# First MLP of a streaming encoder: eight instead of ten hidden pairs done plainly on the first token half, their order, and the places of the operand sums' steps

## The chip, the cores and the metric

One core of a Trainium2 chip. The metric is device time in microseconds of one execution. The kernel before took 2438.1 us, the median of 3 runs (2436.41 to 2440.5).

## The reference

Two trunk layers over 1056 tokens (1024 of a prompt, 32 of a sample), width 1024. Each layer is a mixer (layer 0 an mLSTM, layer 1 chunk-band attention), a residual LayerNorm, an MLP and a residual LayerNorm, with shift, scale and gate from a conditioning vector. The change touches the MLP of layer 0:

```python
x = layer_norm(ALPHA * x + (1 + g1) * y, p['ln_g'][l, 0], p['ln_b'][l, 0])
u = x * (1 + sc2) + sh2
f = jnp.square(jax.nn.relu(u @ p['w_up'][l])) @ p['w_down'][l]
x = layer_norm(ALPHA * x + (1 + g2) * f, p['ln_g'][l, 1], p['ln_b'][l, 1])
```

w_up is 1024 x 4096, w_down 4096 x 1024. All is in 32 bits: every operand is split into a high and a low part, and a product is three matmuls (high-high, high-low, low-high).

## The kernel before

Tokens lie along the free axis, features on the partitions. The 1056 tokens of the MLP are two halves of 528 (`tp` 0 and 1), each two quarters of 264 (QN). The 4096 hidden features are 16 pairs of 256 (`pb`), a pair being two blocks of 128. The upward product is done in two ways (function `mlp7`, lines 1103 to 1533).

*Plain.* For a pair on one half, four tiles (`up_tile`, L1159: block f, quarter q) of 8 k-steps with three matmuls each (`proj`, L118 to L120), 24 matmuls of 128 x 264 columns a tile, 96 a pair. The weights of a pair are two blocks of 512 x 256 (`up_weights`, `wblock`): loaded (L96) into a raw tile, cast to the high part on ScalarE (L89), the low part subtracted on VectorE (L90). ScalarE applies Relu to each tile (L1166), then squares the four (L1141), casts them into HL (L89), VectorE subtracts the low part (L90), and SyncE stores HL to DRAM (`hpl`, L1147).

*In seven products.* A unit (class `Seven`) treats a pair on one half as a 2 x 2 block product with seven multiplications instead of eight: 7 products of 12 matmuls (L1280), 84 a unit. PRODS says what each product multiplies and which of three PSUM tiles of the unit it adds into: the products 0, 2, 4 and 6 add into tile 0, product 1 into tile 1, products 3 and 5 into tile 2. After products 0, 2 and 3 ScalarE copies the PSUM tile to H (L1283), after 1, 4 and 5 VectorE adds it to H (L1286), after 6 ScalarE takes Relu (L1290). The weight forms of a pair (`forms`, four sums L1244 to L1247 of two raw tiles and seven splits, L89 and L90) serve both halves. The operands need sums of quarters of u (`tforms`, L1180): for each half, T3 into `ext` or `exu`, T1 and T2 into TF, and a last difference written in place into U, every step three or two subtractions on VectorE (L1190, L1191, L1195) and a split. It is a generator of six steps; a line in `mlp7` says after which plain tiles a step is taken.

*The order.* Pairs in FIRST (6 to 15) are plain on the first half, which is ready first; the first three of them fill the time in which the second half's LayerNorm ends, the other seven (`rest`) that of the operand sums: a table keyed by `at` (the plain tile pair, counted so that 13 is the last) says which generator moves: 0 or 1 the sums of the first or second half, 2 the weight forms of the first pair. Then come the units in the order of SEQ: a pair of FIRST has one unit (second half), the others two, 22 in all. Two neighbouring units are interleaved: product i of unit j stands at 7j + 2i. While the units run, 8 loads and VectorE work for the adaLN columns of the second layer are spread among them (`ada_some`, L1573, tiles `rada` and `aacc`). Last comes the downward product, in eight groups of two pairs (`dn_plain`), in the order `order_p`.

All raw tiles (weight blocks, `rdn` for the forms, the sums' `t`, `rada`) come from one ring of 3 (`raw_tile`). The weights as used come from a ring of 6 (`wc`), of which `exu` holds one. All DMAs named here are issued by SyncE in one queue. In the rows below a name ends in a buffer number; H_15_0 is pair 15 on half 0, t_0_1 the sum of layer 0, half 1, w_up_15_1 the second weight block of pair 15.

## Time and profile before

| | us |
|---|---|
| median of 3 runs | 2438.1 |
| the profiled execution | 2437.59 |
| its span, first to last instruction | 2435.8 |
| plain part of the first MLP (first matmul 514.0, last 631.4) | 117.5 |
| the 22 units (631.5 to 863.4) | 231.8 |
| TensorE busy | 2363.6 |
| VectorE busy | 1987.5 |
| ScalarE busy | 1178.8 |

The table by stage gives for each stretch the busy time of each engine and its instructions in brackets. The rows in order of time give the start, the duration, the engine, the line, the operation, what it writes and reads, the shape and the count; a bracket at the end is the idle time of the engine before it and what ended it. Matmuls overlap, so their cadence is read from starts. Times are counted from the span's start.

### The profile page before, as it was taken

To read this page: it belongs to the slowest core of one execution; us is meant where nothing else is said; L and a number is where in the kernel's file an instruction comes from. 1 tells how busy PE (TensorE), PEld (TensorE's weight loads), DVE (VectorE), ACT (ScalarE), POOL (GpSimd) and SP (SyncE) were. 2 spreads that over 40 slices of the span, in tenths; PEclk is the share of its full clock that TensorE was granted. 3 is DMA by queue.
4 is the path that set the end of the run, shared out by engine and by line. 5 is a ranking of instruction groups with operands and counts; after the bars stand their busy time and mean duration, and the time that the engine had idled before them with its cause. 6 is when DMAs were issued, how large, how long until landed. Compare 5 with 4: busy or idle time off the path is not lost.

```text
span 2435.8 us, 44452 instructions
## 1 busy us (share of the span) xinstructions
PE 2363.6 (97%) x17180; PEld 2265.8 (93%) x17180; DVE 1987.5 (82%) x4222; ACT 1178.8 (48%) x2394; POOL 166.6 (7%) x315
## 2 busy tenths in 40 slices
PE   7999999999999999999999999999999999899997
PEld 4999999999999999999989977889999999899997
DVE  4899898788788789999697666755998888887778
ACT  4644456278566620010157566763776777222212
POOL 0211100000000000000001134420000000000003
PEclk9999999999999999999999999999999999999999
DMA  8433223436556897656423220051486779966642
GB/s 297 128 103 98 82 86 102 158 113 215 182 186 194 296 343 266 234 203 232 143 64 97 74 64 1 11 133 36 162 279 233 252 255 341 367 242 232 229 151 72
DMA packets 292151, 423.61 MB, mean 174 GB/s; under 512 B 15576, under 2 KB 221804, under 8 KB 286820
## 3 DMA queue, kind: packets, MB, share of 16 engines
q1 hardware_dynamic: 287908, 390.50, 48.3%
q10 hardware_dynamic: 4032, 30.28, 3.1%
q8 instruction: 135, 2.21, 0.4%
q14 instruction: 76, 0.62, 0.1%
HBM read 304.91 MB, written 118.17 MB: 174 GB/s over the span
## 4 chain that ended last, share of the span: by engine, by line
PE 47%; DVE 12%; DMA 5%; ACT 4%; issue 2%; POOL 1%; SPq 0%; DVEq 0%; ACTq 0%; POOLq 0%
PE dn L1415 11%; PE up L1280 9%; PE dn L120 5%; PE dn L119 5%; PE dn L118 5%; PE pv L1853 3%; PE s L1796 2%; PE pt L1831 2%; DMA rdn_u<-in_w_up_dram 1%; DVE wf_u L90 1%; PE op_b L118 1%; PE op_b L119 1%; PE op_b L120 1%; DVE HL L90 1%; DMA radw<-in_w_ada_dram 1%
## 5 line engine op out<-in xcount | busy, mean ns | idle before, releaser
L1045 DVE SCALAR_TENSOR_TENSOR ACX<-dn,ada,ACX 128x264 f32<-128x264 f32 (+6 forms) x664 | 281.9, 448 | 86.4 <-PE dn L1415 41.4
L1415 PE MATMUL dn<-fx,wf_d 128*128 128x264 f32 x2016 | 254.0, 285 | 6.5 <-DVE ACX L1045 3.5
L1415 PEld LDWEIGHTS dn<-fx,wf_d 128*128 128x128 f32 x2016 | 248.7, 188 | 8.7 <-issue 2.5
L89 ACT CAST w_dn<-raw_dn 128x1024 fp32r<-128x1024 f32 x36 | 37.7, 1050 | 284.1 <-DVE aw L274 172.8
L118 PE MATMUL dn<-hs,w_dn 128*128 128x384 f32 (+2 forms) x512 | 161.3, 316 | 0.8 <-DVE ACX L1045 0.7
L119 PE MATMUL dn<-hs,w_dn 128*128 128x384 f32 (+2 forms) x512 | 160.9, 315 | 0.0
L120 PE MATMUL dn<-hs,w_dn 128*128 128x384 f32 (+2 forms) x512 | 155.9, 314 | 1.8 <-DVE w_dn L90 1.8
L1280 PE MATMUL up<-TF,wf_u 128*128 128x264 f32 x1056 | 143.6, 285 | 1.8 <-ACT H L1283 1.8
L1280 PE MATMUL up<-u,wf_u 128*128 128x264 f32 x1056 | 139.7, 285 | 1.7 <-DVE H L1286 0.8
L1280 PE MATMUL up<-U,wf_u 128*128 128x264 f32 x1056 | 139.6, 285 | 1.6 <-DVE H L1286 1.0
L274 DVE SCALAR_TENSOR_TENSOR aw<-radw,cs,aw 128x512 f32<-128x512 f32 x196 | 139.5, 745 | 0.0
L1280 PEld LDWEIGHTS up<-TF,wf_u 128*128 128x128 f32 x1056 | 134.3, 188 | 3.1 <-ACT H L1283 3.0
L1280 PEld LDWEIGHTS up<-U,wf_u 128*128 128x128 f32 x1056 | 133.1, 188 | 2.7 <-DVE H L1286 1.9
L1280 PEld LDWEIGHTS up<-u,wf_u 128*128 128x128 f32 x1056 | 132.6, 188 | 2.7 <-ACT wf_u L89 0.8
L119 PE MATMUL dn<-U,w_dn 128*128 128x384 f32 (+2 forms) x416 | 129.8, 313 | 0.0
L118 PE MATMUL dn<-U,w_dn 128*128 128x384 f32 (+2 forms) x416 | 129.3, 311 | 0.0
L120 PE MATMUL dn<-U,w_dn 128*128 128x384 f32 (+2 forms) x416 | 125.6, 312 | 0.9 <-DVE w_dn L90 0.9
L238 DVE SCALAR_TENSOR_TENSOR ada_room<-ada_room,cs 128x256 f32<-128x256 f32 x224 | 98.9, 476 | 4.2 <-DMA ada_room<-in_w_ada_dram 4.2
L120 PEld LDWEIGHTS dn<-hs,w_dn 128*128 128x128 f32 x512 | 95.8, 188 | 2.9 <-DVE w_dn L90 2.6
L118 PEld LDWEIGHTS dn<-hs,w_dn 128*128 128x128 f32 x512 | 96.4, 188 | 1.5 <-DVE ACX L1045 1.0
L119 PEld LDWEIGHTS dn<-hs,w_dn 128*128 128x128 f32 x512 | 96.5, 188 | 0.0
L1806 DVE CUSTOM_DVE_ANT_0 p<-s,bias 128x576 f32<-128x576 f32 (+9 forms) x132 | 79.1, 606 | 20.3 <-PE s L1796 13.4
(394 smaller groups left out, 7171.5 us busy)
## 6 DMA issues: line engine op xcount, KB each, us to landing
hpl<-HL SPq DMA_DIRECT2D x144, 264.0 KB
rdn_u<-in_w_up_dram SPq DMA_DIRECT2D x64, 512.0 KB
hd<-HL SPq DMA_DIRECT2D x28, 1056.0 KB
fx<-hd SPq DMA_DIRECT2D x50, 528.0 KB
radw<-in_w_ada_dram SPq DMA_DIRECT2D x24, 1024.0 KB
hd<-HM SPq DMA_DIRECT2D x28, 792.0 KB
raw_up<-in_w_up_dram SPq DMA_DIRECT2D x40, 512.0 KB
raw_dn<-in_w_down_dram SPq DMA_DIRECT2D x36, 512.0 KB
```

Source lines behind the costliest of these rows:

```text
L90: (eng or nc.vector).tensor_sub(dst_l, src, dst_h.bitcast(F32))
L118: nc.tensor.matmul(ps, wh, mov(0, k), start=(k == 0), stop=False)
L119: nc.tensor.matmul(ps, wh, mov(1, k), start=False, stop=False)
L120: nc.tensor.matmul(ps, wl, mov(0, k), start=False, stop=(k == nk - 1))
L238: nc.vector.scalar_tensor_tensor(acc[:, cnd], raw[:, k], sc, acc[:, cnd], op0=ALU.mult, op1=ALU.add)
L274: nc.vector.scalar_tensor_tensor(acc[cnd], raw[:, k], sc, acc[cnd], op0=ALU.mult, op1=ALU.add)
L1045: nc.vector.scalar_tensor_tensor(xs, ps[:, off + o:off + o + mm_], gate[:, fc, cnd:cnd + 1], xs, op0=ALU.mult, op1=ALU.add)
L1280: nc.tensor.matmul(p, self.ws[w][:, wl, k], moving(f, tp, xl, k), start=first and k + n_ == 0, stop=k == 3 and n_ == 2, skip_group_check=n ...
L1415: nc.tensor.matmul(p, ws[w][:, wl, k], t[:, s0, xl], start=first and k + n_ == 0, stop=k == kg - 1 and n_ == 2, skip_group_check=not first)
L1796: nc.tensor.matmul(s[:, b, :w], qst, kk[i][:, g, k0 + j0:k0 + j0 + w], start=(i == 0), stop=(i == 1))
L1806: nc.vector.tensor_tensor_reduce(out=z.rearrange("p (b w) -> p b w", b=np_), in0=s[:, :np_, :w], in1=bt.rearrange("p (b w) -> p b w", b=np ...
L1853: nc.tensor.matmul(pv[64 * e:64 * e + 64, :nq], V[:kp, vt0 + j, g * 64:(g + 1) * 64], pts[e][:kp, j, :nq], start=(j == 0), stop=(j == nt - 1))
```

## The change

```diff
@@ -1321,7 +1321,7 @@
-        order_p, blocks_p = (0, 3, 1, 4, 2, 5, 7, 6), [(q * QN, QN) for q in range(4)]
+        order_p, blocks_p = L.order, [(q * QN, QN) for q in range(4)]
@@ -1373,8 +1373,7 @@
                 at = 2 * j + f - 2 * len(rest) + 14
                 if at == 11:
                     prep(0)
-                for n in {2: (1,), 3: (1,), 4: (1,), 5: (1,), 6: (1,), 7: (1,), 8: (0,), 9: (0,), 11: (0, 2),
-                          12: (2,), 13: (2, 0)}.get(at, ()):
+                for n in L.at.get(at, ()):
                     if n < 2:
                         next(tfs[n], None)
@@ -1559,13 +1558,15 @@
     FIRST = [6, 7, 8, 9, 10, 11, 12, 13, 14, 15]
+    FIRST0 = FIRST[2:]
     SEQ = (0, 6, 1, 7, 2, 8, 3, 9, 4, 10, 5, 11, 14, 12, 15, 13)
+    SEQ0 = (0, 8, 1, 9, 2, 3, 10, 4, 5, 6, 7, 11, 14, 12, 15, 13)
     wup0 = {}
     def early_up0(ti, pr):
         if ti == fwd[-1] and pr:
-            wup0[FIRST[pr - 1]] = up_weights(0, FIRST[pr - 1])
+            wup0[FIRST0[pr - 1]] = up_weights(0, FIRST0[pr - 1])
@@ -1588,8 +1589,9 @@
         pairs, quarters = (0, 1), (0, 1, 2, 3)
-        first = FIRST
-        seq = [(pb, (1,) if pb in FIRST else (0, 1)) for pb in SEQ]
+        first, order = FIRST0, (0, 4, 1, 2, 3, 5, 7, 6)
+        at = {5: (1,), 6: (1,), 7: (1,), 8: (1, 1), 9: (1, 0), 10: (0,), 11: (0, 2), 12: (2,), 13: (2, 0)}
+        seq = [(pb, (1,) if pb in FIRST0 else (0, 1)) for pb in SEQ0]
@@ -1997,7 +1999,8 @@
-        first = FIRST
+        first, order = FIRST, ()
+        at = {2: (1,), 3: (1,), 4: (1,), 5: (1,), 6: (1,), 7: (1,), 8: (0,), 9: (0,), 11: (0, 2), 12: (2,), 13: (2, 0)}
```

In layer 0, pairs 6 and 7 are no longer plain on the first half: 8 plain pairs there, 24 units instead of 22. Behind the first three plain pairs stand five instead of seven, that is ten `at` steps (4 to 13) instead of fourteen, and the ten steps of the sums are put on 5 to 13, two at a time at 8 and 9, with the sums of both halves next to each other. The pairs' order among the units has double pairs next to each other (2, 3 and 4, 5, 6, 7), and the groups of the downward product follow it. Layer 1 keeps its tables. The order of instructions on the engines moves with it; three places:

VectorE, around the weights of pair 15, the last plain pair (w_up_15_0 and w_up_15_1), before:

```order
L90 TENSOR_TENSOR U<-t_0_1_6936,U 128x4x264
L90 TENSOR_TENSOR HL_12_0_7124<-H_12_0_7039,HL_12_0_7124 128x4x264
L1195 TENSOR_TENSOR t_0_0_7196<-t_0_0_7196,U 128x1056
L90 TENSOR_TENSOR w_up_15_0_7266<-raw_up_15_0_7264,w_up_15_0_7266 128x1024
L90 TENSOR_TENSOR TF_0_6741<-t_0_0_7196,TF_0_6741 128x1056
L1190 TENSOR_TENSOR t_0_0_7196<-U,t_0_0_7196 128x1056
L1191 TENSOR_TENSOR t_0_0_7196<-t_0_0_7196,U 128x1056
L90 TENSOR_TENSOR w_up_15_1_7271<-raw_up_15_1_7269,w_up_15_1_7271 128x1024
```

The same place with the change:

```order
L1195 TENSOR_TENSOR t_0_0_7010<-t_0_0_7010,U 128x1056
L90 TENSOR_TENSOR w_up_15_0_7016<-raw_up_15_0_7014,w_up_15_0_7016 128x1024
L90 TENSOR_TENSOR TF_1_6742<-t_0_1_6873,TF_1_6742 128x1056
L90 TENSOR_TENSOR HL_13_0_7001<-H_13_0_6912,HL_13_0_7001 128x4x264
L1190 TENSOR_TENSOR t_0_1_6873<-U,t_0_1_6873 128x1056
L90 TENSOR_TENSOR TF_0_6741<-t_0_0_7010,TF_0_6741 128x1056
L1191 TENSOR_TENSOR t_0_1_6873<-t_0_1_6873,U 128x1056
L90 TENSOR_TENSOR w_up_15_1_7021<-raw_up_15_1_7019,w_up_15_1_7021 128x1024
L1190 TENSOR_TENSOR t_0_0_7010<-U,t_0_0_7010 128x1056
L90 TENSOR_TENSOR U<-t_0_1_6873,U 128x4x264
```

Before, the second half's sum (t_0_1) has ended ahead of pair 15's weights; now both sums run on around them, and the second half's last step (U) stands behind.

ScalarE, from the end of the plain part to the copy after product 0 of the first unit (H_0_0 from up_0_0_0), before:

```order
L89 CAST U<-t_0_0_7196 128x4x264
L89 CAST wf_u_0_6_7537<-rdn_u_0_1_7389 128x512
L1166 ACTIVATE H_15_0_7425<-up_15_1_1_7492 128x264
L89 CAST wf_u_6_0_7616<-rdn_u_6_0_7533 128x512
L1141 ACTIVATE H_15_0_7425<-H_15_0_7425 128x1056
L1283 COPY H_0_0_7542<-up_0_0_0_7543 128x264
L89 CAST HL_15_0_7519<-H_15_0_7425 128x4x264
```

And with the change:

```order
L89 CAST wf_u_0_2_7215<-s_u_0_7207 128x512
L89 CAST U<-t_0_0_7010 128x4x264
L89 CAST wf_u_0_2_7215<-s_u_0_7208 128x512
L1166 ACTIVATE H_15_0_7179<-up_15_1_1_7246 128x264
L89 CAST wf_u_0_4_7280<-s_u_0_7209 128x512
L1141 ACTIVATE H_15_0_7179<-H_15_0_7179 128x1056
L89 CAST wf_u_0_4_7280<-s_u_0_7210 128x512
L89 CAST HL_15_0_7273<-H_15_0_7179 128x4x264
L89 CAST wf_u_0_6_7291<-rdn_u_0_1_7143 128x512
L1283 COPY H_0_0_7296<-up_0_0_0_7297 128x264
```

The weight forms of pair 0 (wf_u_0_2, wf_u_0_4), which had stood ahead of these rows, and the cast of HL of pair 15 now stand between the last sum (U) and the copy.

ScalarE, ahead of the copy after product 0 of pair 3's first unit, before (behind pair 8, which has one unit):

```order
L1141 ACTIVATE H_2_1_8379<-H_2_1_8379 128x1056
L89 CAST wf_u_3_4_8653<-s_u_3_8573 128x512
L89 CAST HL_2_1_8632<-H_2_1_8379 128x4x264
L89 CAST wf_u_3_4_8653<-s_u_3_8574 128x512
L1283 COPY H_3_0_8658<-up_3_0_0_8659 128x264
```

And with the change (behind pair 2, which has two):

```order
L1141 ACTIVATE H_2_0_8026<-H_2_0_8026 128x1056
L89 CAST HL_2_0_8249<-H_2_0_8026 128x4x264
L1283 COPY H_2_1_8133<-up_2_1_2_8256 128x264
L89 CAST wf_u_3_4_8273<-s_u_3_8186 128x512
L89 CAST wf_u_3_4_8273<-s_u_3_8187 128x512
L1283 COPY H_3_0_8278<-up_3_0_0_8279 128x264
```

The cast of HL moves ahead of another copy, and the two weight casts stand next to each other. The queue of the first form is before ahead of pairs 2, 3, 4 and 5, with the change ahead of pairs 1 and 2.

## The prediction

> **What bounds the kernel now.** I read the head of the page first, then a table by stage of the first MLP, then TensorE's order of time with its waits, then VectorE, ScalarE and the DMA issues around the one place where the change squeezes them.
>
> ```profile
> span 2435.8 us, 44452 instructions
> PE 2363.6 (97%) x17180; PEld 2265.8 (93%) x17180; DVE 1987.5 (82%) x4222; ACT 1178.8 (48%) x2394; POOL 166.6 (7%) x315
> ```
>
> TensorE is the bound: it is busy for 97% of the span. The profiled execution took 2437.59 us, 1.8 more than its span and 0.5 less than the median of the runs, 2438.1. So matmuls saved count in full, unless another engine then comes late. The stages, with the columns busy time of PE, weight load, DVE, ACT and POOL, granted clock, DMA share and GB/s:
>
> ```profile
> 514.00:631.50 117.50, 117.50 (x966) 117.50 (x965) 90.59 (x112) 90.85 (x159) 0.00 (x0) 1.00 0.55 178
> 631.50:690.00 58.50, 58.50 (x483) 58.50 (x482) 48.16 (x90) 34.72 (x63) 0.00 (x0) 1.00 0.59 187
> 690.00:800.00 110.00, 107.21 (x867) 105.66 (x866) 89.72 (x164) 69.32 (x122) 0.00 (x0) 1.00 0.62 200
> 800.00:863.30 63.30, 62.22 (x513) 61.48 (x512) 47.07 (x78) 44.16 (x77) 0.00 (x0) 1.00 0.90 299
> 561.20:571.60 10.40, 10.40 (x88) 10.40 (x87) 6.30 (x6) 10.40 (x20) 0.00 (x0) 1.00 0.39 131
> 571.60:603.30 31.70, 31.70 (x263) 31.70 (x262) 29.47 (x25) 22.21 (x32) 0.00 (x0) 1.00 0.78 248
> 624.70:631.40 6.70, 6.70 (x57) 6.70 (x56) 0.03 (x1) 1.92 (x4) 0.00 (x0) 1.00 0.48 164
> ```
>
> The first row is the plain part (ten pairs), the next three are the units in seven products. Both are dense at first. What matters are the last three rows, from inside the plain part: up to 571.6 ScalarE is full and VectorE waits for it; then VectorE is 93% busy for 32 us (the operand sums); then it is idle for 6.7 us. That idle time is all the slack which the plain part has, and the change takes 23.5 us of plain matmuls away behind it.
>
> **The direct gain.**
>
> ```profile
> 631.53 3.08 PE L1280 MATMUL up<-U,wf_u 128*128 128x264 f32 x24
> 634.45 3.08 PE L1280 MATMUL up<-TF,wf_u 128*128 128x264 f32 x24
> 637.37 1.61 PE L1280 MATMUL up<-U,wf_u 128*128 128x264 f32 x12
> 863.37 0.28 PE L118 MATMUL dn<-U,w_dn 128*128 128x264 f32 x1
> ```
>
> A plain pair is 4 tiles of 24 matmuls; ten pairs are 960 in 117.5 us, 0.1224 each. A unit is 84 matmuls at 2.92 / 24 = 0.1217. Two pairs go (192 x 0.1224 = 23.5 us), two units come (168 x 0.1217 = 20.4): **-3.1 us**. With the pairs go 4 weight loads, 4 copies on ScalarE and 4 subtractions on VectorE; the units add 6 sums on VectorE. All of that lies beside TensorE in stages where it is the longest, so I price it at nothing by itself; its effect on waits is the next two terms.
>
> **The waits among the units.** 22 units are 1848 matmuls, 224.7 us at 0.1217, but they take 863.37 - 631.53 = 231.8: 7.1 us are lost. The idle time is 2.79 us in 690 to 800 and 1.08 behind it, so I put 7.1 x 2.79 / 3.87 = 5.1 us of the loss into the middle.
>
> ```profile
> 727.51 1.73 PE L1280 MATMUL up<-U,wf_u 128*128 128x264 f32 x12 [0.43 <-DVE H L1286]
> 758.47 1.73 PE L1280 MATMUL up<-TF,wf_u 128*128 128x264 f32 x12 [0.91 <-ACT H L1283]
> 770.98 1.73 PE L1280 MATMUL up<-U,wf_u 128*128 128x264 f32 x12 [0.55 <-DVE H L1286]
> 791.03 1.72 PE L1280 MATMUL up<-TF,wf_u 128*128 128x264 f32 x12 [0.77 <-ACT H L1283]
> ```
>
> Counted by products, the second and fourth row are the third product of pairs 4 and 5 on the first half, the third row the seventh of pair 4, the first row the seventh of the unit ahead of pair 3: all where a double pair follows a single one. There the copy of the first product (L1283) is queued on ScalarE behind two weight casts with the cast of HL between them; the order before has that queue ahead of pairs 2, 3, 4 and 5. The new order has it ahead of 1 and 2 and a milder one ahead of 4; four of the eight double pairs (3, 5, 6, 7) follow a double one, where the copy stands as it does ahead of the single pairs, which do not wait. I take **-3.0 us**; the ends are 0 (the waits only move) and -5.1 (all gone). The tail, five single pairs at the same place before the end, keeps its loss.
>
> **The start of the units.** This is the price. Rows of VectorE, ScalarE and the DMA queue around it:
>
> ```profile
> 571.66 2.36 DVE L90 TENSOR_TENSOR w_up<-raw_up,w_up 128x1024 fp32r<-128x1024 f32 x2 [1.91 <-ACT w_up L89]
> 589.14 1.22 DVE L90 TENSOR_TENSOR w_up<-raw_up,w_up 128x1024 fp32r<-128x1024 f32 x1
> 594.04 1.22 DVE L90 TENSOR_TENSOR w_up<-raw_up,w_up 128x1024 fp32r<-128x1024 f32 x1
> 595.18 1.25 DVE L1190 TENSOR_TENSOR t<-U,t 128x1056 f32<-128x1056 f32 x1
> 596.35 1.25 DVE L1190 TENSOR_TENSOR t<-U 128x1056 f32<-128x1056 f32 x1
> 620.03 0.39 ACT L1166 ACTIVATE H<-up 128x264 f32<-128x264 f32 x1
> 620.32 0.61 ACT L89 CAST wf_u<-s_u 128x512 fp32r<-128x512 f32 x1
> 620.83 1.09 ACT L1141 ACTIVATE H<-H 128x1056 f32<-128x1056 f32 x1
> 606.48 4.83 SPq L1228 DMA_DIRECT2D rdn_u<-in_w_up_dram  x2
> 611.75 0.62 ACT L89 CAST wf_u<-rdn_u 128x512 fp32r<-128x512 f32 x1 [0.59 <-DMA rdn_u<-in_w_up_dram]
> 633.55 0.37 ACT L1283 COPY H<-up 128x264 f32<-128x264 f32 x1
> 633.80 1.08 ACT L89 CAST HL<-H 128x1056 fp32r<-128x1056 f32 x1
> ```
>
> Durations, start to start: a subtraction of 1056 columns 1.17 (595.18 to 596.35), of a weight half 1.14 (594.04 to 595.18), of 512 columns 0.6 (an estimate from its half size); on ScalarE a cast of 512 columns 0.5, of 1056 about 1.0, a tile's Relu 0.3. A load of 512 KB takes 5.3 (issued 606.48, used 611.75).
>
> All queues stand as before up to the fifth pair's weights at 571.66, since ScalarE has its 10.4 full us there in both. From there the new VectorE queue has, to the second half of pair 15's weights, 6 weight halves and 17 full subtractions: 6.8 + 19.9 = 26.7, hence 598.4. Pair 15 is now the eighth plain pair; TensorE reaches it at 514.0 + 7 x 11.75 = 596.3 and needs that half 1.5 us later, at 597.8. Before, the eighth pair's half was ready at 590.3 (589.14). The two operand tiles of both halves are now live at once and leave one of three raw tiles to the weights, so the two loads of pair 15 go one after the other: issue at 592.6, used at 597.9, cast, subtracted at 599.6. TensorE waits 1.8 there. In SyncE's queue the stores of pair 13's HL and the forms' loads stand behind that second load; the stores end before the next HL is cast, at 600.4.
>
> That subtraction frees the raw tile for pair 0's first forms: load 599.6 to 604.9, cast to 605.5, and then on VectorE three of 512 and three of 1056 columns with 0.6 of waiting: 611.4. Now ScalarE's queue ends it: behind that sum stand the cast of U (1.0), four casts of 512 columns (2.0), Relu, Square and the cast of HL of pair 15 (2.3), and only then the copy of pair 0's first product (0.35): 5.7 us, 617.1. Before, that copy stood ahead of HL and was done at 633.9, in time for the third product at 634.45. The third product adds into the same PSUM tile, so it waits for this copy: it would start at 514.0 + 8 x 11.75 + 2.9 = 610.9 and starts at 617.1 or a little later: **+6.3 us**, the 1.8 within it. Behind TensorE in that wait is everything. If no load is waited for, VectorE reaches the sum at 608.4 and the loss is 3.2; if each of the two loads in a row takes 1 us more, it is 8.3. I take 6.3, since 5.3 is a measured load and all the rest are queue lengths.
>
> **The clock behind it.** TensorE would idle from 612.7 to 617.1, 4.4 us in one piece. The trace has such a gap elsewhere, in the stage of the q projection:
>
> ```profile
> 1261.00:1262.00 1.00, 0.00 (x0) 0.00 (x0) 0.97 (x3) 0.18 (x1) 0.00 (x0) 1.00 0.00 0
> 1264.00:1265.00 1.00, 0.37 (x1) 0.00 (x1) 0.94 (x3) 0.00 (x0) 0.00 (x0) 0.50 0.39 135
> 1269.00:1270.00 1.00, 1.00 (x5) 1.00 (x5) 0.00 (x1) 0.48 (x1) 0.00 (x0) 0.50 0.00 0
> 1271.00:1272.00 1.00, 1.00 (x7) 1.00 (x6) 1.00 (x2) 0.00 (x0) 0.00 (x0) 1.00 0.00 0
> ```
> ```profile
> 1256.65 0.34 PE L119 MATMUL q<-U,w_q 128*128 128x384 f32 x1
> 1256.83 0.34 PE L120 MATMUL q<-U,w_q 128*128 128x384 f32 x1
> 1259.99 0.34 PE L120 MATMUL q<-U,w_q 128*128 128x384 f32 x1
> 1265.03 0.66 PE L118 MATMUL q<-U,w_q 128*128 128x384 f32 x1 [0.66 <-DVE QO L1677]
> 1266.44 0.53 PE L119 MATMUL q<-U,w_q 128*128 128x384 f32 x1
> 1266.76 0.53 PE L120 MATMUL q<-U,w_q 128*128 128x384 f32 x1
> ```
>
> From 1260.3 to 1265.0 hardly anything ran; then the granted clock is 0.50 until after 1270, and matmuls come every 0.32 instead of 0.18 us: of some 5.3 us 2.4 are lost. I take **+2.4 us** (ends 0, if 4.4 us is too short, and 2.6). The Trainium skill, TensorE: Matmul & The Clock Gate, section HAM oscillation — how this bites in real kernels, asks for no idle gap over about 3.4 us, and halves the clock behind one until TensorE has been busy as long: an estimate of 1.7 us here, and 2439.6 for the sum. The trace agrees with the halving and shows it longer.
>
> **The sum.** -3.1 - 3.0 + 6.3 + 2.4 = +2.6 us: 2440.2 by the profiled execution, 2440.7 by the median. I say 2440.5.
>
> **Rivals.**
> - *The start is covered.* If ScalarE comes to the copy before 610.9, only -3.1 - 3.0 is left: 2431.5. For it: the walk adds up some 40 instructions, and 0.15 us less on each would take it away. Against it: even with no load waited for, it ends 3.2 late.
> - *No fall of the clock.* The wait is there but broken up by pair 15's 1.8, or shorter than what trips the clock: 2437.8.
> - *Slower: the raw tiles.* Three of them carry weight loads, operand sums and the loads of the adaLN columns. If loads, not the queue behind HL, make the copies late among the units, the waits only move to other pairs and the -3.0 is not had: 2443.2, and 2445.2 with the start at its upper end. It decides from the point at which the first forms of a pair land later than the unit before last ends; the DMA share of 0.59 to 0.62 there speaks against it; for it, what VectorE waited for such loads from 514 to 863 (us in all, times, longest):
>
> ```profile
> DVE s_u L1244 <- DMA rdn_u<-in_w_up_dram: 14.1, 7, 4.9
> ```
>
>
> **How the numbers follow.** Forecast 0.45, no fall of the clock 0.22, raw tiles 0.20, covered 0.13. A measurement of this kernel tells about 0.2% from no change, 4.9 us: faster is below 2433.2, slower above 2443.0. Faster gets most of the covered case, 0.10; slower three quarters of the raw tiles and a tenth of the forecast, 0.20; same 0.70. All ends together give 2432.3 to 2445.7; the range 2434 to 2445 leaves out the bulk of the covered case and the outermost of the slow one.
>
> **What would show it.** Right: a gap of 4 to 6 us on TensorE at the third product of the first unit, put down to ACT H L1283; a granted clock of 0.5 for some 5 us behind it; VectorE without an idle stretch in the 10 us before; waits of about 2 us in all among the units up to the single pairs at the end; plain part plus units 3.1 us shorter without waits. Wrong: the first units dense, as before, or a wait there on a weight load; or new waits at pairs 4 to 7.

## The result, and the profile after

The changed kernel takes **2442.64 us**, the median of 17 runs (2439.16 to 2446.2), against 2438.1 in 17 runs of the kernel before (2433.29 to 2441.81): a ratio of 1.0019 (95% interval 1.0012 to 1.0025), 4.5 us slower by the medians. The prediction said 2440.5. The profiled execution took 2441.56 us, 3.97 more than that of before. The head of its page:

```profile
span 2439.7 us, 44392 instructions
PE 2361.6 (97%) x17156; PEld 2265.7 (93%) x17156; DVE 1984.3 (81%) x4224; ACT 1178.7 (48%) x2392; POOL 167.1 (7%) x315
```

TensorE is busy 2.0 us less and the span is 3.9 longer, so 5.9 us went into idling. The table by stage (columns as before the change: PE, weight load, DVE, ACT, POOL, granted clock, DMA share, GB/s) has the plain part, three pieces of the units, and then two short stretches at the first unit:

```profile
513.13:608.19 95.06, 94.41 (x774) 94.19 (x773) 77.04 (x98) 77.40 (x138) 0.00 (x0) 1.00 0.51 169
608.19:690.00 81.81, 77.45 (x613) 76.82 (x612) 64.80 (x116) 49.33 (x87) 0.00 (x0) 0.96 0.56 177
690.00:800.00 110.00, 107.21 (x878) 106.19 (x878) 82.04 (x152) 65.09 (x113) 0.00 (x0) 1.00 0.58 186
800.00:865.90 65.90, 65.51 (x539) 65.30 (x538) 48.96 (x80) 46.84 (x82) 0.00 (x0) 1.00 0.89 296
611.30:614.90 3.60, 0.00 (x0) 0.00 (x0) 3.60 (x6) 3.60 (x7) 0.00 (x0) 0.80 0.50 146
615.00:620.30 5.30, 5.30 (x24) 5.30 (x25) 4.32 (x8) 1.33 (x3) 0.00 (x0) 0.50 0.91 301
```

The fifth row is a hole: no matmul, VectorE and ScalarE full. In the sixth 24 matmuls take 5.3 us at half the clock; a unit's 24 take 2.92 elsewhere. All rows of TensorE from 500 to 866 that name a wait:

```profile
598.09 0.39 PE L120 MATMUL up<-U,w_up 128*128 128x264 f32 x1 [0.65 <-DVE w_up L90]
614.97 5.43 PE L1280 MATMUL up<-TF,wf_u 128*128 128x264 f32 x23 [3.70 <-ACT H L1283]
678.43 1.72 PE L1280 MATMUL up<-TF,wf_u 128*128 128x264 f32 x12 [0.59 <-ACT H L1283]
690.71 1.74 PE L1280 MATMUL up<-U,wf_u 128*128 128x264 f32 x12 [0.35 <-DVE H L1286]
727.74 0.50 PE L1280 MATMUL up<-U,wf_u 128*128 128x264 f32 x2 [0.23 <-ACT wf_u L89]
729.74 0.51 PE L1280 MATMUL up<-U,wf_u 128*128 128x264 f32 x2 [1.50 <-DVE wf_u L90]
734.87 1.72 PE L1280 MATMUL up<-U,wf_u 128*128 128x264 f32 x12 [0.71 <-DVE H L1286]
862.90 3.17 PE L1280 MATMUL up<-U,wf_u 128*128 128x264 f32 x24 [0.39 <-ACT H L1283]
```

(A count below 12 or 24 here and in later fences, such as x23 and x2, ends with the window in which the rows were read, at 620 or 730.) The second row is the stall that the prediction described: the third product of the first unit, put down to the copy of L1283. The rows at 727 to 735 belong to pair 4 and are new. The waits of before at 758, 771 and 791 are gone.

To compare runs I take the stage from the first plain matmul to the first matmul of the downward product (865.91 here), and split what it loses against dense matmuls (0.1224 us each in a plain pair, 0.1217 in a unit, as in the prediction). After: the plain part takes 95.06 for 768 x 0.1224 = 94.0, so 1.0 is lost; the third product starts at 614.97 instead of 608.19 + 24 x 0.1217 = 611.11, a gap of 3.9; its 24 matmuls up to 620.38 take 5.41 instead of 2.92, 2.5 more; and of the units' 257.72 us 245.35 are matmuls, so 257.72 - 245.35 - 3.9 - 2.5 = 6.0 is lost in all other units.

| us | before | after | predicted | measured |
|---|---|---|---|---|
| matmuls of the stage | | | -3.1 | -3.1 |
| plain part and gap of the first unit | 0 | 1.0 + 3.9 | +6.3 | +4.9 |
| half clock behind it | 0 | 2.5 | +2.4 | +2.5 |
| all other units | 6.9 | 6.0 | -3.0 | -0.9 |
| the stage | 349.4 | 352.8 | +2.6 | +3.4 |

The -3.1 in the last column is the count of matmuls at the dense cadence, not a reading of its own. The other 0.6 of the 3.97 us lies outside this stage, where the change moves only the order of the downward product's groups; what lies there differs by more than that from one profile to the next (below). The half clock came out as forecast, the start a little cheaper, and the relief among the units hardly came.

ScalarE ahead of the copy, in order of time:

```profile
609.26 1.08 ACT L89 CAST U<-t 128x1056 fp32r<-128x1056 f32 x1 [0.60 <-DVE t L1191]
610.25 0.62 ACT L89 CAST wf_u<-s_u 128x512 fp32r<-128x512 f32 x1
...
611.56 1.08 ACT L1141 ACTIVATE H<-H 128x1056 f32<-128x1056 f32 x1
612.54 0.61 ACT L89 CAST wf_u<-s_u 128x512 fp32r<-128x512 f32 x1
613.05 1.07 ACT L89 CAST HL<-H 128x1056 fp32r<-128x1056 f32 x1
614.02 0.62 ACT L89 CAST wf_u<-rdn_u 128x512 fp32r<-128x512 f32 x1
614.54 0.37 ACT L1283 COPY H<-up 128x264 f32<-128x264 f32 x1
```

(The dots stand for a Relu and a cast.) From the cast behind VectorE's sum (609.26) to the copy's end (614.91) ScalarE has no idle time: 5.65 us of queue, where the prediction counted 5.7. The gap is shorter than predicted because that sum ended at 609.1, not at 611.4.

### The profile page after: what moved, and what is told of

It reads as the page before. It is cut to its first block, busy times and chain, and to the rows that moved or that the text cites. A ratio compares the mean times of both kernels' runs of the same rounds, so it can differ in the third digit from the quotient of the medians.

```text
span 2439.7 us, 44392 instructions
## 1 busy us (share of the span) xinstructions
PE 2361.6 (97%) x17156; PEld 2265.7 (93%) x17156; DVE 1984.3 (81%) x4224; ACT 1178.7 (48%) x2392; POOL 167.1 (7%) x315
## 3 DMA queue, kind: packets, MB, share of 16 engines
q8 instruction: 135, 2.21, 0.4%
## 4 chain that ended last, share of the span: by engine, by line
PE 62%; DVE 17%; DMA 7%; ACT 5%; issue 3%; SPq 1%; POOL 0%; DVEq 0%; ACTq 0%; POOLq 0%
PE dn L1414 11%; PE up L1280 9%; PE dn L120 5%; PE dn L119 4%; PE dn L118 4%; PE pv L1855 3%; PE s L1798 2%; DMA rdn_u<-in_w_up_dram 2%; PE pt L1833 2%; DVE wf_u L90 2%; DVE HL L90 1%; DMA hpl<-HL 1%; PE op_a L118 1%; PE op_a L119 1%; PE op_a L120 1%
## 5 line engine op out<-in xcount | busy, mean ns | idle before, releaser
L1280 PE MATMUL up<-TF,wf_u 128*128 128x264 f32 x1104 | 152.3, 288 | 5.6 <-ACT H L1283 5.6
L1280 PE MATMUL up<-U,wf_u 128*128 128x264 f32 x1152 | 152.6, 285 | 3.3 <-DVE wf_u L90 1.5
L1280 PEld LDWEIGHTS up<-U,wf_u 128*128 128x128 f32 x1152 | 145.4, 188 | 4.6 <-DVE H L1286 1.8
L1280 PEld LDWEIGHTS up<-TF,wf_u 128*128 128x128 f32 x1104 | 142.6, 191 | 7.1 <-ACT H L1283 7.1
L90 DVE TENSOR_TENSOR HL<-H,HL 128x1056 fp32r<-128x1056 f32 x64 | 80.3, 1254 | 23.9 <-ACT HL L89 23.9
```

What stands on the lines that cost most here:

```text
L90: (eng or nc.vector).tensor_sub(dst_l, src, dst_h.bitcast(F32))
L1280: nc.tensor.matmul(p, self.ws[w][:, wl, k], moving(f, tp, xl, k), start=first and k + n_ == 0, stop=k == 3 and n_ == 2, skip_group_check=n ...
```

## The experiments

Every run was made beside runs of the kernel before on the same chip; the ratio is to those, with its 95% interval. As with the change itself, an edit can move the order of instructions on the engines around it; where that bears on a reading it is said. The columns between are read from one profile each, split as above ("gap" holds the spare matmuls too, where there are any; "behind" is what the next 27 matmuls lose, by the half clock or by further waits, since in some runs the half clock reaches into the fourth product; by this split before loses 6.9 among its units, where the prediction had 7.1).

| run | plain part | gap | behind | other units | stage | ratio |
|---|---|---|---|---|---|---|
| before | 0 | 0 | 0 | 6.9 | 349.4 | |
| after | 1.0 | 3.9 | 2.5 | 6.0 | 352.8 | 1.0019 (1.0012 to 1.0025) |
| e1 copy first | 0.9 | 2.6 | 1.6 | 7.1 | 351.6 | 1.0003 (0.9994 to 1.0012) |
| e2 spare matmuls | 1.3 | 4.4 | 0.1 | 7.8 | 352.9 | 1.0009 (1.0000 to 1.0018) |
| e3 ten pairs, steps closer | 0 | 0 | 0 | 8.4 | 350.9 | 0.9998 (0.9990 to 1.0007) |
| e4 tile for the sums | 0.1 | 2.3 | 2.1 | 6.3 | 350.2 | 0.9997 (0.9988 to 1.0006) |
| e5 tile for adaLN | 1.5 | 3.7 | 2.8 | 1.2 | 348.5 | 1.0002 (0.9993 to 1.0010) |
| e6 alternating order | 2.1 | 4.6 | 2.1 | 6.4 | 354.6 | 1.0042 (1.0028 to 1.0056) |
| e7 nine pairs | 0.1 | 3.5 | 2.7 | 3.3 | 350.5 | 1.0024 (1.0013 to 1.0035) |
| e8 e1 + a tile for both | 0.1 | 1.8 | 4.1 | 0.6 | 346.0 | 0.9988 (0.9979 to 0.9996) |
| e9 before + tile for adaLN | 0 | 0 | 0 | 4.2 | 346.6 | 0.9992 (0.9983 to 1.0001) |
| e10 HL on GpSimd | 3.1 | 4.4 | 2.5 | 0.7 | 350.0 | 1.0016 (1.0007 to 1.0025) |
| e11 e5 + spare matmuls | 0.9 | 4.3 | 0.1 | 1.6 | 346.2 | 1.0004 (0.9995 to 1.0012) |
| e12 e8 + spare matmuls | 0.1 | 2.9 | 0.3 | 1.5 | 344.1 | 0.9979 (0.9970 to 0.9988) |

From the first matmul of the downward product to the last of all, profiles of kernels that differ there at most in the order of the groups lie several us apart: 1560.9 before, 1562.1 after, and with the order of after 1556.1 (e4) to 1563.2 (e5); e7 has 1569.6, with waits that are named below. A ratio alone therefore doesn't show a step of 1 or 2 us; the stage does, though each stage is read from one profile.

### The start: which queue, and why it is late

**e1, the copy ahead.** Theory Q is the prediction's: ScalarE's queue behind a late VectorE.

```diff
+            late = not NW and pb == L.first[-1]
-            if hts[pb, tp][1] == 4:
+            if hts[pb, tp][1] == 4 and not late:
...
                 sevens[j].product(i, up_end if j == len(jobs) - 1 else None)
+                if not NW and (j, i) == (0, 1):
+                    h_forms(L.first[-1], tp0, hts.pop((L.first[-1], tp0))[0])
```

> One edit on the changed kernel: the Square and the HL cast of pair 15, the last plain pair on the first half, are issued behind the first unit's second product instead of ahead of its first. Theory Q (queue on ScalarE): the third product waits for the copy of the first, and that copy stands behind this Square and cast after a sum that VectorE ends at 609.1. With them out of the way four casts of 512 columns remain between the cast of U (610.25) and the copy, so the copy ends near 613.0 instead of 614.9, the gap of TensorE is 1.9 us instead of 3.9, and a gap that short leaves the clock at 1.00: 1.9 + 2.5 less, 2438.2 us by the median of 2442.6. Rival R (raw tiles: the loads come late): the third product waits for a weight form instead and starts at 614 or later, gap and clock as they are, 2442.

```profile
615.03 4.70 PE L1280 MATMUL up<-TF,wf_u 128*128 128x264 f32 x24 [2.43 <-ACT H L1283]
```

The plain part starts 1.46 us later here than after the change (514.59 against 513.13), so the product comes 1.4 us sooner, and its wait has the same name. The two operations last 2.0 us between them and were worth 1.4, the sum having ended 0.5 us later here; what is left ahead of the copy is that sum, its cast, a Relu and four casts. 2.6 us of gap still brought the half clock, for a shorter time, so of the two gains expected only a part came. The stage is 1.2 us shorter than after the change; the median, 2439.33, is 3.3 lower, more than the stage explains, but the intervals of the two ratios leave room for both.

**e4, a tile of their own for the sums.**

```diff
-                return raw_tile([P, 4, QN], f"t{i}_{l}_{tp}")
+                return hhp.tile([P, 4, QN], F32, tag="tt", name=f"t{i}_{l}_{tp}", bufs=1) if not NW else raw_tile([P, 4, QN], f"t{i}_{l}_{tp}")
```

> One edit on the changed kernel: the operand sums have a tile of their own instead of two of the three raw tiles, so that the weight loads and the first forms' loads have all three. Rival R: the loads of pair 15 and of pair 0's forms come early, the 0.65 us wait in pair 15 and the gap at the third product go, and with them the fall of the clock: 2436 us. Theory Q: VectorE is full from 571 to 612 whatever the loads do (it waited 1.0 us for them in all from 596), so the sum ends about 1 us earlier, the wait in pair 15 goes, the gap is still some 2.5 us: 2440.5 us, or 2438 if that gap no longer trips the clock.

```profile
615.55 0.39 PE L1280 MATMUL up<-TF,wf_u 128*128 128x264 f32 x1 [2.13 <-ACT H L1283]
616.17 4.18 PE L1280 MATMUL up<-TF,wf_u 128*128 128x264 f32 x22 [0.23 <-DVE TF L90]
```

The wait in pair 15 goes and the gap shrinks to 2.3, as Q said; it still trips the clock, and it doesn't go as R said. The stage is 2.6 us shorter than after the change, as in Q's 2440.5; the median, 2437.83, is lower by more than that, and Q's lower figure was meant for a clock at 1.00, so this time alone decides nothing. Among the units of this run the half clock came a second time, at pair 4 (last section), which is a part of its 6.3. ScalarE's order moved with this edit too: HL's cast and the four casts stand no longer between the last sum's cast and the copy, and what is left ahead of the copy is a cast of TF, for which ScalarE waited 1.74 us on VectorE's sum, and a Square. So the raw tiles are a part of the start's lateness (0.9 + 1.6 us), not all of it.

**e3, ten pairs with the closer steps.** `FIRST0 = FIRST`, `SEQ0 = SEQ`, the old group order, the new table.

> One part of the change alone: ten plain pairs and the units in the order of before, with only the operand sums' steps closer together (the new table). Theory Q: what hurts is that the sums' last 50 us begin while ScalarE is still full (up to 571); with ten pairs they begin behind it, at about 579, so VectorE is done 3 us or more ahead of the first unit's third product and nothing waits: 2438 us as before, within 1. Rival K: the closer steps themselves are the cost, whatever the number of pairs: a gap of 3 to 4 us at the third product of the first unit and the half clock behind it, 2444 us.

2438.08 us, the first unit dense, no half clock. The closer steps alone cost nothing at the start: Q. ScalarE's order ahead of the copy is that of before here. (Its units lose 8.4 where before loses 6.9, which I did not take apart.) VectorE sits idle for 2.69 us just before its last sum's subtraction:

```profile
631.48 1.26 DVE L90 TENSOR_TENSOR U<-t,U 128x1056 fp32r<-128x1056 f32 x1 [2.69 <-ACT U L89]
```

**e7, nine pairs.** FIRST from 7 on, order 0 7 1 8 2 9 3 6 10 4 11 5 14 12 15 13, steps on 3 to 13.

> Half the change: nine plain pairs, 23 units, the sums' steps over eleven half pairs instead of nine. Theory Q with VectorE as the one that is late: a plain pair gives VectorE 11.75 us and takes 4 x 1.2 = 4.7 of it, so the ninth pair brings it 7 us, more than the 3.9 of the gap and the 0.7 in pair 15: the first unit is dense, no half clock, and half of the direct gain stays: -1.55 us, 2436.5, and waits among the units as in one of the two. Rival K (the closer steps by themselves): the gap stays at 3 us or more and the half clock with it, 2442.

Q missed. The gap and the half clock are there as K forecast (3.5 us; 2443.60 where it said 2442), though VectorE has room: it waits 2.21, 1.15 and 1.75 us ahead of 603.7, 611.4 and 625.2. But K's reason, the closer steps by themselves, is not what the rows show. ScalarE ahead of the copy:

```profile
621.73 0.40 ACT L1166 ACTIVATE H<-up 128x264 f32<-128x264 f32 x1
624.50 0.62 ACT L89 CAST wf_u<-rdn_u 128x512 fp32r<-128x512 f32 x1 [2.37 <-DMA rdn_u<-in_w_up_dram]
625.02 1.08 ACT L1141 ACTIVATE H<-H 128x1056 f32<-128x1056 f32 x1
626.01 0.36 ACT L1283 COPY H<-up 128x264 f32<-128x264 f32 x1
```

The cast of the second pair's first form stands ahead of the copy, and its load came late: 2.4 us of waiting for a DMA, in the same queue. SyncE issued that load at 620.09, just behind the stores of an HL (617.44 to 619.98), whose subtraction VectorE had ended at 617.4; whether SyncE's order or VectorE's put it there was not tested. So Q holds for the place (ScalarE's queue ahead of the copy), but VectorE need not be what fills it. The stage is 2.3 us shorter than after the change; behind it, in this profile, the downward product waits for weights at 890 and 906 (1.7 and 3.7 us, the second with the half clock behind it), which I did not take apart.

**e10, HL's subtraction on GpSimd.** On e5's and e1's edits:

```diff
-                split(hl[:, :, 0], hl[:, :, 1], H[:, 0:4])
+                split(hl[:, :, 0], hl[:, :, 1], H[:, 0:4], nc.gpsimd if not NW and tp == tp0 and pb in L.first[-4:] else None)
```

> Three edits on the changed kernel: the adaLN columns have their own tile, the Square and the HL cast of pair 15 stand behind the first unit's second product, and the HL subtractions of the last four plain pairs (1056 columns, 1.17 us each on VectorE, three of them between 571 and 612) run on GpSimd, which has nothing else to do there. Theory Q (VectorE is the one that is late): its sum ends 3.5 us earlier, at 605.6 instead of 609.1, the copy is done before the third product is due at 611.1, the gap and the half clock go. Then of the 7.4 us lost at the start under 1 remains and the middle is dense: 2442.6 - 6.5 - 4.6 = 2431.5 us. If GpSimd is slow (no subtraction of this size is in the trace; from 1.2 to some 6 us), the HL stores come later, and ScalarE's next HL cast waits for the one tile of HL: the gap stays at 1 to 2.6 us as with the copy's edit alone: 2434 to 2435 us.

It missed on the other side: 1.0016, the start worse (3.1 in the plain part, a gap of 4.4). The rows of GpSimd, and of VectorE at the same time:

```profile
584.73 2.56 POOL L90 TENSOR_TENSOR HL<-H,HL 128x1056 fp32r<-128x1056 f32 x1 [215.37 <-ACT HL L89]
606.42 2.56 POOL L90 TENSOR_TENSOR HL<-H,HL 128x1056 fp32r<-128x1056 f32 x1 [8.70 <-ACT HL L89]
```
```profile
583.71 1.25 DVE L90 TENSOR_TENSOR TF<-t,TF 128x1056 fp32r<-128x1056 f32 x1
584.88 3.53 DVE L1191 TENSOR_TENSOR t<-t,U 128x1056 f32<-128x1056 f32 x1
606.69 3.41 DVE L1190 TENSOR_TENSOR t<-U,t 128x1056 f32<-128x1056 f32 x1
```

A subtraction of 1056 columns takes VectorE 1.25 us, and 3.5 when it starts just behind one of GpSimd: 584.73 + 2.56 + 1.25 = 588.54, and it ends at 588.41. VectorE stood until GpSimd was done. Each of the three subtractions moved ahead of the gap took 1.2 us of work from VectorE and made it stand 2.2 to 2.3.

### The clock

**e2, spare matmuls in the gap**, into a tile that nobody reads.

```diff
+                spare = mm("spare0")[:, :QN] if not NW and (j, i) == (0, 1) else None
+                for s_ in range(0 if spare is None else 30):
+                    nc.tensor.matmul(spare, got[0][0][:, 0, s_ % 4], moving(PRODS[0][1], tp0, 0, s_ % 4), start=s_ == 0, stop=s_ == 29)
```

> One edit on the changed kernel: 30 spare matmuls of 264 columns, into a tile of their own that nobody reads, between the second and the third product of the first unit: 30 x 0.1217 = 3.65 us, about the 3.7 us for which TensorE waits there. Theory Q with the clock's fall as a cost of its own: the third product starts at 615 as before, the granted clock stays 1.00, and the 2.5 us that the half clock costs go: 2440.1 us. Rival: the fall of the clock costs nothing by itself, because VectorE and ScalarE would hold the next products as late anyway: 2442.6, with new waits of some 2.5 us between 615 and 625.

The clock stayed at 1.00, and the 24 matmuls behind lose 0.1 instead of 2.5. The median, 2439.07, is within the first theory's reach; but in this profile the stage is no shorter, since waits of 0.8 and 0.4 us stand at 847 and 853 that the changed kernel lacks (before has one of 0.6 at 849), and the plain part and the gap are 0.8 longer together. Undecided by itself, so it was repeated where nothing else waits.

**e11, the same on e5.**

> Two edits on the changed kernel: the adaLN columns have their own tile, and 30 spare matmuls stand between the second and the third product of the first unit. With the waits among the units gone, what the clock costs can be read by itself against the run with the adaLN tile alone (2438.0 us; 6.5 us lost at the start, of it 3.7 gap and 2.5 half clock). Clock as a cost of its own: no half clock, the start loses some 4.4 us, nothing is lost behind it: 2436 us. Rival (VectorE and ScalarE are late anyway): waits of about 2 us come up between the third and the fourteenth product, 2438 us.

The row of e5 behind its gap, and the same length in e11:

```profile
617.00:622.30 5.30, 5.30 (x24) 5.30 (x25) 4.32 (x8) 1.32 (x3) 0.00 (x0) 0.50 0.94 302
```
```profile
617.95:623.25 5.30, 5.30 (x43) 5.30 (x44) 4.88 (x9) 2.02 (x5) 0.00 (x0) 1.00 0.96 304
```

24 against 43 matmuls in 5.3 us, and behind it no row names a wait until 859: the stage is 2.2 us shorter than e5's (346.2 against 348.5). Of that, 0.5 lies in the plain part, ahead of the spare matmuls; from the first unit on it is 1.7. The clock is a cost of its own, though not all of the 2.7 that the split shows comes back: the gap is 0.5 longer and the later units lose 0.5 more. The ratios (1.0004 and 1.0002) can't tell the two apart.

### Among the units

**e5, a tile of their own for the adaLN columns.** The new wait at pair 4 led to this: of SyncE's loads for pair 4, one was issued at 723.35, when VectorE's work on an adaLN tile had just ended, and VectorE then stood for it:

```profile
722.84 0.48 DVE L238 SCALAR_TENSOR_TENSOR aacc<-rada,cs,aacc 128x256 f32<-128x256 f32 x1
727.07 0.69 DVE L1244 TENSOR_TENSOR s_u<-rdn_u,rdn_u 128x512 f32<-128x512 f32 x1 [3.75 <-DMA rdn_u<-in_w_up_dram]
```

```diff
+        L.own = lambda shape, name: hhp.tile(shape, F32, tag="own", name=name, bufs=1)
...
-        yield from ada_cols(a["w_ada_kv"], 0, 96, 8, mm, tmp_t, ADA_B)
+        yield from ada_cols(a["w_ada_kv"], 0, 96, 8, mm, tmp_t, ADA_B, L0.own)
```

> One edit on the changed kernel: the loads of the adaLN columns among the units have a tile of their own instead of one of the three raw tiles. In the changed kernel the largest new wait among the units is at pair 4's first product (0.23 + 1.50 us at 727 to 730, and 0.71 behind it at 735): one of pair 4's two loads is issued at 723.35, when VectorE has just ended its last multiplication on the adaLN columns (from 722.84). Theory R2 (the raw tile of the adaLN columns delays pair 4's forms): the two waits at 727 to 730 and the one at 735 go, 3.1 us with the matmuls' restart, and the start stays as it is: 2439.5 us of 2442.6. Rival S: the loads are late because two double pairs and a single one follow each other, whoever holds the third tile: the waits stay within 0.5 us, 2442.

All rows of e5 from 500 to 866 that name a wait:

```profile
600.19 0.39 PE L120 MATMUL up<-U,w_up 128*128 128x264 f32 x1 [1.07 <-DVE w_up L90]
616.96 3.45 PE L1280 MATMUL up<-TF,wf_u 128*128 128x264 f32 x14 [3.58 <-ACT H L1283]
860.24 3.23 PE L1280 MATMUL up<-U,wf_u 128*128 128x264 f32 x24 [0.47 <-ACT H L1283]
```

Not only the waits of pair 4 are gone but all between the first unit and the last, the one on ScalarE's copy at 678 (0.59) too. 4.8 us of 6.0: R2, and more than the 3.1 that it expected. What VectorE waited for the forms' loads from 630 to 850 (us in all, times, longest), after the change and in e5:

```profile
DVE s_u L1244 <- DMA rdn_u<-in_w_up_dram: 13.8, 6, 3.9
```
```profile
DVE s_u L1244 <- DMA rdn_u<-in_w_up_dram: 5.5, 3, 3.4
```

At pair 4 TensorE itself waited for such forms, so there the third raw tile is the cause. For the waits at pair 2 it is not the only candidate, since ScalarE's order changed as well: after the change a weight cast, HL's cast, a second weight cast and the copy follow each other at 676.01, 676.51, 677.49 and 678.01; in e5 HL's cast comes first (675.52), then both weight casts (676.50) and the copy (677.55). Late forms and the queue went together there.

**e6, the order undone** (`SEQ0 = (0, 8, 1, 9, 2, 10, 3, 11, 4, 5, 6, 7, 14, 12, 15, 13)` and the groups to match).

> One part of the change undone: eight plain pairs and the new table, but double and single pairs alternate up to pair 3 (0 8 1 9 2 10 3 11 4 5 6 7 14 12 15 13), and the four double pairs in a row stand at the end of them. If the new order gives the relief that the prediction took, this one has the waits of before back, at the pairs 2, 3 and 4, and is 2 to 3 us slower than the changed kernel: 2445 us. If the relief is as small as the changed kernel's trace shows (6.0 us lost beside the start against 7.1 before), and its largest wait belongs to pair 4 behind 2, 3, 10, then that wait moves or goes and the time is 2441 to 2443 us. The start, gap and half clock, is the same in both.

2446.62 us looks like the relief undone, but the profile puts it elsewhere: other units lose 6.4 against 6.0; 1.8 lies in the plain part and at the gap, and 1.0 and 2.1 us are waits for weights in the downward product, with a half clock behind the second. Pair 4's wait for its forms is gone, and in its place the third product of pair 4 waits 0.89 us for the copy again, as before the change. As long as the raw tiles are shared, the order moves the waits and is worth 0.4 us among the units.

**e9, the kernel before with the tile.**

> The kernel before with one edit: the adaLN columns among the units have a tile of their own (ten plain pairs, its own order and its own table). In the changed kernel that edit took all waits among the units away (from the second unit to the last one but one TensorE lost nothing) and 4.6 us by the median. Theory R2 (the waits among the units come from the raw tile that the adaLN columns take, in any order of the pairs): of the 6.9 us that the kernel before loses among its units about 1 remains at the very end, and nothing at the start: 2438.1 - 5.5 = 2432.6 us. Rival O (the order of before has waits of its own, where a double pair follows a single one and two weight casts with the cast of HL stand ahead of the copy, as the prediction said): the waits at the pairs 3, 4 and 5 stay, 2437 us or more.

```profile
771.15 1.74 PE L1280 MATMUL up<-U,wf_u 128*128 128x264 f32 x12 [0.22 <-DVE H L1286]
832.56 1.75 PE L1280 MATMUL up<-TF,wf_u 128*128 128x264 f32 x12 [0.58 <-ACT H L1283]
```

In between. The waits of before at 727, 758 and 791 are gone, the one at 771 fell from 0.55 to 0.22, and 6.9 became 4.2. VectorE waits 6.8 us for the forms' loads from 630 to 850 here, and 14.1 before. But the queue that the prediction named, HL's cast between two weight casts, is gone ahead of pairs 2 to 5 too: at pair 4 HL's cast comes first here (755.52), then both weight casts (756.50) and the copy (757.54). So this run doesn't tell late forms from the queue either. Three smaller waits are new, at 685, 697 and 833 (0.46, 0.23 and 0.58), and the last unit's stays. 4.2 remain, against 1.2 in e5; whether that is the order or the number of pairs is not separated. By the ratio the gain is about 2 us with zero at the edge of its interval: not the 5.5 that R2 expected.

### Together

**e8**: e1's edit, and one tile for both the sums and the adaLN columns.

> Three edits on the changed kernel together: operand sums and adaLN columns share one tile of their own, so that the three raw tiles hold weights alone, and the Square and HL cast of pair 15 stand behind the first unit's second product. If gap (copy behind HL), raw tiles at the start and adaLN tile among the units are separate causes, their gains add up: of the 7.4 us that the changed kernel loses at its start 1.3 remain, with the clock at 1.00, and the 3.1 at pair 4 go: 9 us less, 2433.5 us, ahead of the kernel before. If they are one cause (VectorE is full whatever the tiles do), the start gains what the copy's edit alone gained, 3.3 by the median, and the middle little: 2438 to 2439 us.

2435.49 us, 0.9988: faster than the kernel before. The middle is dense (0.6). At the start the copy comes sooner (gap 1.8), and then, as the second row says, a sum is late. Probably that is because all sums share one tile: VectorE subtracts the last TF at 612.94 here and at 614.87 in e4, where they share one too, but at 604.38 after the change.

```profile
612.65 0.39 PE L1280 MATMUL up<-TF,wf_u 128*128 128x264 f32 x1 [1.65 <-ACT H L1283]
614.25 5.43 PE L1280 MATMUL up<-TF,wf_u 128*128 128x264 f32 x23 [1.20 <-DVE TF L90]
```

**e12**: e8 with 24 spare matmuls at e2's place.

> The three edits of the run with one tile for sums and adaLN columns and the later HL of pair 15, and 24 spare matmuls (2.9 us) between the second and the third product of the first unit, where that run waited 3.3 us and then had the half clock. If the clock is a cost of its own, as the run with the adaLN tile and spare matmuls showed between plain part and down projection (2.2 us less there), then here too: no half clock behind the first unit, 3.4 instead of 5.9 us lost at the start, nothing behind it, 343.6 us from the first plain matmul to the first of the down projection, and a ratio to the kernel before of 0.998. If the spare matmuls only move the wait, the stage stays at 346.0 us and the ratio at 0.999.

2431.97 us, **0.9979** (0.9970 to 0.9988), the fastest here, 344.1 us for the stage where 343.6 was expected. The stage is 1.9 us shorter than e8's, and that difference lies behind the start of the first unit. From 610 on only one row names a wait in the stage:

```profile
856.72 3.23 PE L1280 MATMUL up<-U,wf_u 128*128 128x264 f32 x24 [0.48 <-ACT H L1283]
```

This stage is 2.5 us shorter than that of ten pairs with an adaLN tile (e9). That is near the 3.1 that the matmuls give, but not a measurement of it: the two still lose 4.8 and 4.2 us, in different places, and ten pairs with a tile for the sums as well were not run.

## Why the prediction was right, and where not

- **Direct gain, -3.1:** as forecast, by the matmuls' count; no run isolates it. The cadence that it rests on holds: in e5, where no row from 617 to 860 names a wait, the units from 627 to 760 run at 0.1217 us a matmul.
- **Start, +6.3, measured +4.9:** the mechanism is right, shown by e1 (two operations less in the queue, product 1.4 us sooner, same releaser) and e3 (no gap where VectorE has idle time). Of the 4.9, 2.5 go with a tile for the sums (e4), the share of the raw tiles, which the prediction had in its walk as two loads one after the other. A late load can hold up the same queue where VectorE has room (e7). The size is off by 1.4: the walk had VectorE's sum end at 611.4, it ended at 609.1. The plain part began 0.9 us earlier, pair 15's second block was done at 598.0 instead of 599.6 (0.7 sooner, counted from the plain part's start), and the way from there to the sum took 11.1 us instead of 11.8. The wait in pair 15 was 0.65 instead of 1.8.
- **Clock, +2.4, measured +2.5:** right, and a price of its own and not part of the wait; taking it away gave 1.7 us (e11 against e5, from the first unit on) and 1.9 (e12 against e8).
- **Waits among the units, -3.0, measured -0.9:** this step failed, by a term that it put at nothing, late loads of the forms. Counted from the starts of the matmuls, before loses 5.1 us from pair 2 to pair 5, where the queue with HL's cast between two weight casts stood, and after the change 1.9 remain at pairs 1 and 2, where it stands now: 3.2 less, near the forecast. The single pairs at the end, which were to keep their loss, lose 0.6 instead of 1.8. But 3.1 came anew at pair 4, where TensorE waited for the forms themselves (1.50 us on VectorE's part of one), whose load came late because the adaLN columns held one of three raw tiles (e5), and 0.4 at pair 6. That was the rival "the raw tiles, the waits only move", and its sign in the prediction, new waits at pairs 4 to 7, is what came. It was held down to 0.20 by the DMA share of 0.59 to 0.62, which says how busy the DMA engines are and nothing on who holds a tile. The row quoted for it, VectorE waiting 14.1 us for `rdn`, was the one to follow: after the change it is 13.8, in e5 5.5. The time alone doesn't choose: counted from the median of before the forecast is 2440.7 and the rival 2443.7, and 2442.64 lies between. Whether the queue makes waits by itself, as the prediction had it, stays open: the adaLN tile took the waits and the queue away together (e5, e9), and the same queue stood ahead of pairs 2 and 3 before and ahead of pair 1 after the change without a wait of 0.15 us or more at the third product.
- That the forecast fell only 2 us from the result is in part luck: a start priced 1.4 too high stood against a relief priced 2.1 too high. The remaining part, 0.6 in the profile and about 1 by the medians, lies outside the stage and is not explained.
- Three small sums of the prediction are off, without weight for the forecast: 1848 x 0.1217 is 224.9 and leaves a loss of 6.9, the sum with 1.7 us for the clock is 2439.8, and the lowest of all ends is 2432.9.

## What to carry to other kernels

A wait's releaser names the last instruction of a queue; before pricing a new order by that queue, ask what the instructions ahead of it waited for, back to the load and to whoever held its buffer. After an edit, compare the order on the engines as well as the waits before naming the cause: a tile of its own changed both here. A buffer ring shared by a paced background task and the critical loads turns into waits that wander with every reordering: give the task a tile of its own first, then compare orders. When a change makes one stage shorter, the work that lay hidden in it is the first thing to price, and a hole on TensorE has to be counted with the half clock that may follow it: behind holes of 3.3 us and more it came each time in these traces, behind shorter ones down to some 1.5 in this MLP sometimes. Spare matmuls in the hole kept the clock up in the three runs that had them.

## What the runs showed of the hardware

**The half clock comes in steps, and behind a short hole by chance.** One-us rows of the changed kernel, then of e1, with the granted clock behind the brackets:

```profile
613.00:614.00 1.00, 0.00 (x0) 0.00 (x0) 1.00 (x2) 1.00 (x2) 0.00 (x0) 0.74 0.45 156
620.00:621.00 1.00, 1.00 (x9) 1.00 (x9) 1.00 (x3) 0.38 (x1) 0.00 (x0) 0.84 0.87 236
```
```profile
614.00:615.00 1.00, 0.00 (x0) 0.00 (x0) 1.00 (x3) 1.00 (x4) 0.00 (x0) 1.00 0.93 287
615.00:616.00 1.00, 0.97 (x4) 0.97 (x5) 1.00 (x2) 0.96 (x1) 0.00 (x0) 0.50 0.49 172
618.00:619.00 1.00, 1.00 (x9) 1.00 (x8) 1.00 (x1) 0.38 (x1) 0.00 (x0) 0.79 0.78 255
```

A mean of 0.74 is half a clock for 0.52 of that us, so after the change it lasts from 613.48 to 620.32, 6.8 us; in e1 from 615.0 to 618.42, 3.4 us, half as long. In all these traces the stretches at half the clock between 90 and 2100 us last 3.4 or 6.8 us, four times longer (10.2 and 13.7).

Waits of 2.13 (e4) and 2.43 us (e1) at the first unit were enough, and with spare matmuls, with waits of 0.6 us and less left, it did not come. In between it is not the length alone that decides. Pair 4 waits for the same form in both of these rows, after the change and in e4, and only in e4 the clock falls behind it:

```profile
731.00:732.00 1.00, 1.00 (x10) 1.00 (x10) 1.00 (x2) 0.78 (x2) 0.00 (x0) 1.00 0.99 342
```
```profile
731.00:732.00 1.00, 1.00 (x7) 1.00 (x6) 1.00 (x2) 0.08 (x1) 0.00 (x0) 0.50 0.50 176
```

The wait ahead of them is 1.50 us in both. One of 3.06 us in the q projection brought the half clock in the changed kernel (at 1255) and not in e1 (at 1255), and one of 2.69 us in pair 15 of e10 did not either; all of 3.3 us and more did. A single profile therefore can have such a loss or lack it, e1's and e4's at the first unit too. The Trainium skill, TensorE: Matmul & The Clock Gate, section HAM oscillation — how this bites in real kernels, asks for no gap over about 3.4 us; the runs show that a shorter one can cost as well.

**GpSimd and VectorE take turns** on subtractions with both inputs in SBUF (e10: 1.25 us became 3.5 behind one of GpSimd of 2.56; and one of GpSimd that started at 594.16, 0.02 us behind one of VectorE, took 3.56). The Trainium skill, SBUF — State Buffer, section Who interferes with whom, says that such a VectorE instruction waits for a GpSimd instruction that reads SBUF, or the other way round, whichever is first; these rows agree in both directions.
